# Residual projection in 512-column pieces, inverse roots by a GpSimd power, gate weight splits two blocks later, last gate parts of 512, 384 and 128 columns

## The chip, the cores and the metric

The kernel runs on one core of a Trainium2 chip. The metric is the device time of one execution in microseconds (us), the median of several executions. The engines are named as in the profile: PE is the matrix engine (PEld its weight loads), DVE the vector engine, ACT the scalar engine, POOL the GpSimd engine, and SP the engine whose queue starts most of the transfers.

## The reference, cut to what matters

512 tokens of width 1024 go through one block. The residual stream is `h`.

```python
xn = rms_norm(h, g_mix)
proj = xn @ w_in                                  # 1024 -> 2048
h = h + concat([y_conv, y_pool]) @ w_o            # the residual projection, 1024 -> 1024
h = h + peer_ffn(rms_norm(h, g_ffn), ...)         # 16384 experts, top 16 per head and token
gate = sigmoid(rms_norm(h, g_ple) @ w_ple_gate)   # the gate, 1024 -> 1024
h = h + gate * (p @ w_ple_proj)
return rms_norm(h, g_final)

def rms_norm(x, g):
    return x * rsqrt(mean(x * x) + 1e-6) * g
```

`rms_norm` occurs four times for every token. Each time it needs one inverse root per token, so one column of 128 numbers for a tile of 128 tokens.

## The kernel before, in words

Tokens are in 4 tiles of 128. Almost every product is made of three matmuls: both operands are split into a rounded high part and a low part (`xH`, `xL`), and `mm3` adds high by high, high by low and low by high in one accumulator (lines L126, L130 and L128). A split (`split_ld`, L98) is a copy on ACT (L99) and a subtraction on DVE (L100).

The program runs in this order.

- **Start.** `h` is loaded and `norm_rows` scales the four tiles by their inverse root. Four small projections of `p` (`ple`, L190) run on PE meanwhile, then `h` is transposed and the input projection `w_in` begins. This part is in the order in which it is written (a manual schedule).
- **Middle, in an order that a scheduler chooses.** The rest of `w_in`, the convolution and the pooling, which leave their result in `mixH` and `mixL`. Then the **residual projection** (L307 to L319): `w_o` comes in four pieces of 256 columns by all eight chunks of 128 rows. Every piece is loaded to `wraw`, split to `wH` and `wL` (two buffers each), and used for the four token tiles, 24 matmuls of 256 columns each, after which DVE adds the accumulator to `h`. Four more `ple`, the norm of the new `h`, its transposes, the query projection, the top-k search, and the scores of experts (accumulators `acc`) follow.
- **Expert values, written by hand in order again.** From L795 on, a loop over 128 blocks of 128 experts. Block `n` is multiplied into six accumulators `o` (three token tiles by two halves, 18 matmuls of 512 columns). The loop body prepares later blocks: ACT and DVE split the expert weights `wH`, `wL` of block `n + 2` and the rows `vH`, `vL` of block `n + 2`, and SP loads `vraw` of block `n + 5`. The fourth token tile does not use this path: POOL gathers its 256 rows of experts one at a time (L540, indirect DMA) and DVE adds them (L564). In blocks 76 to 104 of this loop the gate weight comes in as eight chunks: `gate_dma` (L731) loads one chunk to `tH` (two buffers) at the end of every fourth block, and `gate_split` (L741) splits it one block later (L862).
- **Tail.** For the four tiles in the order 3, 0, 1, 2: `tail_norm` (norm), `tail_T` (transposes), `tail_gate` (gate projection in parts, sigmoid on ACT, product and sum on DVE, square sum on ACT for the last norm) and `tail_out` (inverse root, scaling, store). Three tiles do the gate in two parts of 512 columns (`HS`), the last one in three of 512, 256 and 256 (`QS`, L747).

The **inverse root** (`rsqrt`, L102) is one ACT square root, then a reciprocal and one Newton step in four DVE operations on 128x1. Before it, DVE turns the sum of squares into the mean plus epsilon (L118, and L907 or L909 in the tail). In the tail ACT changes between the tables of the square root and of the sigmoid. In the last part of the last tile a dummy square root (L900) brings its table load ahead of the square.

ACT, DVE and PE take their instructions in order, so an instruction that waits holds back everything behind it on its engine.

Of the kernel before, what the change touches and what calls it, by code (L numbers as in the profile page):

```python
# [7 lines left out]
F32 = mybir.dt.float32  # L8
# [8 lines left out]
P = 128  # L17
# [37 lines left out]

SEGS = [(0, 1, 16), (1, 1, 8), (2, 1, 5), (3, 1, 4), (4, 1, 3), (5, 3, 2), (8, 8, 1)]
NCAND = sum(n * b for _, n, b in SEGS)


@with_exitstack  # L60
def block_kernel(ctx: ExitStack, tc: tile.TileContext, x, pT_in, g_cols, w_in, conv_w, pool_w,
# [31 lines left out]
    eidx = consts.tile([P, P], I32, name="eidx")  # L93
    gate3 = consts.tile([P, P], F32, name="gate3")
    xrow = consts.tile([P, D], F32, name="xrow")
    consts.tile([P, 64], F32, name="lpad")

    def split_ld(src, hi, lo):  # L98
        nc.scalar.activation(hi, src, AF.Copy)  # L99
        nc.vector.tensor_tensor(lo, src, hi.bitcast(F32), op=OP.subtract)  # L100

    def rsqrt(ms):  # L102
        sq = small.tile([P, 1], F32, name="sq")
        nc.scalar.activation(sq, ms, AF.Sqrt)
        r = small.tile([P, 1], F32, name="r")
        nc.vector.reciprocal(r, sq)
        t = small.tile([P, 1], F32, name="nt")
        nc.vector.scalar_tensor_tensor(t, r, ms, r, op0=OP.mult, op1=OP.mult)
        nc.vector.tensor_scalar(t, t, -0.5, 1.5, op0=OP.mult, op1=OP.add)
        r2 = small.tile([P, 1], F32, name="r2", bufs=4)  # L110
        nc.vector.tensor_tensor(r2, r, t, op=OP.mult)
        return r2

    def rstd(src, scratch):
        ss = small.tile([P, 1], F32, name="ss")
        nc.scalar.activation(scratch, src, AF.Square, accum_out=ss)
        ms = small.tile([P, 1], F32, name="ms")
        nc.vector.tensor_scalar(ms, ss, 1.0 / D, EPS, op0=OP.mult, op1=OP.add)  # L118
        return rsqrt(ms)

    def mm3(ps, lh, ll, rh, rl, start, stop):
        mm3_pair([(ps, lh, ll, rh, rl)], start, stop)
# [43 lines left out]
    def piece_hl():  # L166
        return (wpool.tile([P, DC, 256], F32R, name="wH"), wpool.tile([P, DC, 256], F32R, name="wL"))

    def piece(w, c0):
        raw = piece_dma(w, c0)  # L170
        hl = piece_hl()
        split_ld(raw, *hl)
        return hl
# [27 lines left out]
    start.enter_context(tc.manual_schedule())  # L201
    warm = consts.tile([P, 1], F32, name="warm")
    nc.vector.memset(warm, 1.0)
    nc.scalar.activation(warm, warm, AF.Sqrt)
    ple_w(0)
    nc.sync.dma_start(h[:, 0], x[:P])
    ident = const("ident", ident_in, [P, P])
# [67 lines left out]
    for k, pc in enumerate(order):  # L275
        w = pieces.pop(pc)
        if 0 < k < len(order) - 1:
            pieces[order[k + 1]] = piece(w_in, order[k + 1] * 256)
        elif k:
            pieces["o0"] = piece(w_o, 0)  # L280
        both = projT(w, xh, xl) if k else first
        for b in range(2):
            ps = both[b]
            blk = 2 * pc + b
            kind, g = divmod(blk, 4)
            if kind == 3:
                pool_group(g, ps)
            elif kind == 1:
                cbuf[g] = wk.tile([P, T], F32, name="cb")
                nc.scalar.activation(cbuf[g], ps, AF.Copy)  # L290
            elif kind == 2:
                z = wk.tile([P, T + 2], F32, name="zb", bufs=1)
                nc.vector.memset(z[:, 0:1], 0.0)
                nc.vector.memset(z[:, T + 1:], 0.0)
                nc.vector.tensor_tensor(z[:, 1:T + 1], cbuf[g], ps, op=OP.mult)
                y = wk.tile([P, T], F32, name="yb")
                nc.vector.tensor_scalar(y, z[:, 0:T], cw[:, g, 0:1], None, op0=OP.mult)
                nc.vector.scalar_tensor_tensor(y, z[:, 1:T + 1], cw[:, g, 1:2], y, op0=OP.mult, op1=OP.add)
                nc.vector.scalar_tensor_tensor(y, z[:, 2:T + 2], cw[:, g, 2:3], y, op0=OP.mult, op1=OP.add)
                zbuf[g] = y  # L300
            else:
                m = wk.tile([P, T], F32, name="cm", bufs=1)
                nc.vector.tensor_tensor(m, zbuf[g], ps, op=OP.mult)
                split_ld(m, mixH[:, g], mixL[:, g])

    corder = [4, 5, 6, 7, 0, 1, 2, 3]
    for qd in range(4):  # L307
        w = pieces.pop("o%d" % qd)
        if qd < 3:
            pieces["o%d" % (qd + 1)] = piece(w_o, (qd + 1) * 256)  # L310
        else:
            pieces["q0"] = piece(w_q, 0)
        for t in range(NT):
            ps = psum.tile([P, T], F32, name="acc", bufs=4)
            ts = slice(t * P, (t + 1) * P)
            for ci, c in enumerate(corder):
                mm3(ps[:, :256], mixH[:, c, ts], mixL[:, c, ts], w[0][:, c], w[1][:, c], ci == 0, ci == DC - 1)
            hs = h[:, t, qd * 256:(qd + 1) * 256]
            nc.vector.tensor_tensor(hs, hs, ps[:, :256], op=OP.add)  # L319

    for t in range(NT):
        ple(t, 1)
# [421 lines left out]
            split_ld(raw[:, hf * 512:(hf + 1) * 512], *wg(hf, c))  # L744

    HS = [slice(0, 512), slice(512, 1024)]
    QS = [slice(0, 512), slice(512, 768), slice(768, 1024)]  # L747
    st_t, fin_t = {}, {}

    def tail_norm(t):  # L750
# [44 lines left out]
    for n in range(NE - LAST):  # L795
        m = n + LAG
        i = n - NS
        if m < NR:
            r = RATES[0]
        elif m < NG:  # L800
            r = RATES[1]
        elif m < NS:
            r = RATES[2]
        else:
            if left is None:
                left = 2 * P - done[0]
# [36 lines left out]
        gather(max(0, q - 2))  # L843
        if fu:
            gelu(m, ps)
            if m % 2:
                w_mult(m - 1)
                w_h(m - 1)
                w_l(m - 1)
        if n == NE - LAST - 1:  # L850
            for k in range(n + LAG + 1, NE):
                w_mult(k)
                w_h(k)
                w_l(k)
            for k in range(n + 3, NE):
                v_h(k)
                v_l(k)
            tail_norm(ND)
        mix(n, range(ND))
        if 16 <= i < 48 and i % 4 == 0:  # L860
            gate_dma((i - 16) // 4)
        if 17 <= i < 49 and i % 4 == 1:  # L862
            gate_split((i - 16) // 4)
        if i == 48:
            nc.sync.dma_start(gpb, bcast(g_ple))
            nc.sync.dma_start(gfin, bcast(g_final))
# [17 lines left out]
    def tail_gate(t, bank, parts, obuf):  # L884
# [1 line left out]
        sg = wq.tile([P, D], F32, name="aq")  # L886
        o_ = vb.tile([P, D], F32, name=obuf)
        ss = small.tile([P, 3], F32, name="ss2")
        m0 = None
        for n, s in enumerate(parts):  # L890
            hf, o = divmod(s.start, 512)
            w = s.stop - s.start
# [3 lines left out]
                mm3(ps, hi[:, c], lo[:, c], wh[:, o:o + w], wl[:, o:o + w], c == 0, c == DC - 1)  # L896
            yield
            nc.scalar.activation(sg[:, s], ps, AF.Sigmoid)
            if n == len(parts) - 1 == 2:
                nc.scalar.activation(warm, warm, AF.Sqrt)  # L900
            nc.vector.tensor_tensor(sg[:, s], sg[:, s], pl[:, s], op=OP.mult)
            nc.vector.tensor_tensor(sg[:, s], sg[:, s], h3[:, s], op=OP.add)
            nc.scalar.activation(ps, sg[:, s], AF.Square, accum_out=ss[:, n:n + 1])
            nc.vector.tensor_tensor(o_[:, s], sg[:, s], gfin[:, s], op=OP.mult)
            m1 = small.tile([P, 1], F32, name="ms3", bufs=6)
            if n == 0:
                nc.vector.tensor_scalar(m1, ss[:, 0:1], 1.0 / D, EPS, op0=OP.mult, op1=OP.add)  # L907
            else:
                nc.vector.scalar_tensor_tensor(m1, ss[:, n:n + 1], 1.0 / D, m0, op0=OP.mult, op1=OP.add)  # L909
            m0 = m1  # L910
        fin_t[t] = o_, m0

    def tail_out(t):
        o_, ms_ = fin_t[t]
        r = rsqrt(ms_)
        nc.vector.tensor_scalar(o_[:, HS[0]], o_[:, HS[0]], r, None, op0=OP.mult)
        nc.sync.dma_start(out[t * P:(t + 1) * P, HS[0]], o_[:, HS[0]])
        if t < ND - 1 or t == ND:
# [84 lines left out]
```

## Time and profile before

| what | value |
|---|---|
| median of 3 runs | 1442.31 us (1441.92 to 1448.14) |
| the profiled execution's own time | 1441.66 us |
| its span, from the first to the last instruction | 1439.9 us |
| PE busy | 1421.2 us (99%) |
| DVE busy | 1137.6 us (79%) |
| ACT busy | 613.1 us (43%) |
| POOL busy | 381.2 us (26%) |
| granted TensorE clock, mean | 0.998 of 2.4 GHz |

The span is 1.8 us shorter than the execution's own time, and that execution is 0.65 us under the median of the runs. Matmuls overlap in the profile: a 512-column one is shown with 390 ns, while the next starts 227 ns later. What PE can do is therefore read from the distance between starts.

### The profile page before, as it was taken

The page shows a single profiled execution, that of the slowest core. Times are in us where ns is not written, and L with a number is a line of the kernel's source. Part 1 is how long each engine was busy: PE and PEld are TensorE (multiplying, and loading weights), DVE is VectorE, ACT ScalarE, POOL GpSimd, SP SyncE. Part 2 cuts the span into 40 slices and gives each one's busy share as a digit, 9 for nine tenths or more (in the row PEclk, how much of TensorE's full clock was granted, in tenths as well). Part 3 has the DMA queues.
Part 4 walks back from the last instruction along what each step waited for, and adds up shares of the span by engine and source line. Part 5 has one row for each costly group of instructions (what it writes and reads, how often), then busy time and mean ns, then how long its engine had stood idle before and what let it go on. Part 6 is the DMA issues. An engine that isn't in the chain of part 4 may idle for free.

```text
span 1439.9 us, 20603 instructions
## 1 busy us (share of the span) xinstructions
PE 1421.2 (99%) x7785; PEld 1268.5 (88%) x7785; DVE 1137.6 (79%) x2078; ACT 613.1 (43%) x864; POOL 381.2 (26%) x260
## 2 busy tenths in 40 slices
PE   8999999999999999999999999999999999999997
PEld 5789888999999999998999999999998888778886
DVE  5653679899999988869988779887887777777665
ACT  5321533344565666663333333333333333334345
POOL 0000000002121241116766456444443123332000
PEclk9999999999999999999999999999999999999999
DMA  8233730158688989989998989898878989998621
GB/s 293 88 102 103 254 113 30 31 182 293 218 300 304 312 296 319 292 314 329 384 360 324 380 310 371 330 344 331 337 280 310 330 311 338 330 331 321 242 72 73
DMA packets 152083, 380.99 MB, mean 265 GB/s; under 512 B 10928, under 2 KB 72240, under 8 KB 151728
## 3 DMA queue, kind: packets, MB, share of 16 engines
q1 hardware_dynamic: 72400, 211.36, 41.3%
q0 software_dynamic: 36864, 134.23, 25.5%
q10 hardware_dynamic: 42720, 34.08, 7.2%
q8 instruction: 61, 1.00, 0.3%
q14 instruction: 38, 0.31, 0.1%
HBM read 339.53 MB, written 40.11 MB: 264 GB/s over the span
## 4 chain that ended last, share of the span: by engine, by line
PE 92%; DVE 3%; DMA 3%; issue 1%; ACT 1%; SPq 0%; DVEq 0%
PE acc L128 13%; PE acc L130 12%; PE acc L126 12%; PE o L130 11%; PE o L128 11%; PE o L126 11%; PE u L130 5%; PE u L126 5%; PE u L128 5%; DMA tH<-in_w_gate 2%; PE g L474 2%; PE g L475 2%; DVE vL L608 1%; PE acc L194 1%; PE tp L520 1%
## 5 line engine op out<-in xcount | busy, mean ns | idle before, releaser
L540 POOL DMA_INDIRECT gr<-in_u_rows,eidx x128 | 198.0, 1547 | 640.3 <-DVE tsm L393 329.9
L540 POOL DMA_INDIRECT gr<-in_v_rows,eidx x128 | 183.0, 1430 | 294.9 <-DVE xrow L564 284.3
L128 PE MATMUL o<-vL,wH 128*128 128x512 f32 x768 | 237.8, 391 | 1.4 <-DVE vL L608 1.4
L126 PE MATMUL o<-vH,wH 128*128 128x512 f32 x768 | 238.2, 391 | 1.0 <-ACT wH L691 1.0
L130 PE MATMUL o<-vH,wL 128*128 128x512 f32 x768 | 238.0, 391 | 0.8 <-DVE wL L696 0.6
L602 ACT ACTIVATE vH<-vraw 128x1024 fp32r<-128x1024 f32 x128 | 135.3, 1058 | 216.6 <-PE o L130 170.0
L608 DVE TENSOR_TENSOR vL<-vraw,vH 128x1024 fp32r<-128x1024 f32 x128 | 156.3, 1221 | 64.0 <-ACT vH L602 63.9
L128 PE MATMUL acc<-xL,uH 128*128 128x384 f32 x608 | 206.1, 339 | 0.0
L126 PE MATMUL acc<-xH,uH 128*128 128x384 f32 x608 | 204.1, 336 | 0.0
L130 PE MATMUL acc<-xH,uL 128*128 128x384 f32 x608 | 203.6, 335 | 0.0
L584 ACT ACTIVATE uH<-uraw 128x1024 fp32r<-128x1024 f32 x128 | 135.1, 1057 | 124.6 <-PE acc L128 105.6
L128 PEld LDWEIGHTS o<-vL,wH 128*128 128x128 f32 x768 | 144.3, 188 | 33.2 <-DVE vL L608 2.3
L130 PEld LDWEIGHTS o<-vH,wL 128*128 128x128 f32 x768 | 144.3, 188 | 32.6 <-DVE wL L696 2.2
L590 DVE TENSOR_TENSOR uL<-uraw,uH 128x1024 fp32r<-128x1024 f32 x128 | 155.4, 1217 | 20.8 <-ACT uH L584 20.3
L126 PEld LDWEIGHTS o<-vH,wH 128*128 128x128 f32 x768 | 143.5, 188 | 28.4 <-ACT wH L691 1.8
L564 DVE SCALAR_TENSOR_TENSOR xrow<-gr,gate,xrow 128x1024 f32<-128x1024 f32 x128 | 164.2, 1283 | 5.1 <-DMA xrow<-h_d 4.6
L560 DVE SCALAR_TENSOR_TENSOR gr<-gr,xrow 128x1024 f32<-128x1024 f32 x128 | 154.2, 1216 | 4.5 <-DMA gr<-in_u_rows,eidx 4.5
L130 PE MATMUL u<-xH,uL 128*128 128x384 f32 x416 | 139.6, 336 | 0.0
L126 PE MATMUL u<-xH,uH 128*128 128x384 f32 x416 | 139.6, 336 | 0.0
L128 PE MATMUL u<-xL,uH 128*128 128x384 f32 x416 | 139.3, 335 | 0.0
L130 PEld LDWEIGHTS acc<-xH,uL 128*128 128x128 f32 x608 | 114.3, 188 | 0.0
L128 PEld LDWEIGHTS acc<-xL,uH 128*128 128x128 f32 x608 | 114.2, 188 | 0.0
(214 smaller groups left out, 2329.6 us busy)
## 6 DMA issues: line engine op xcount, KB each, us to landing
uraw<-in_u_blk SPq DMA_DIRECT2D x128, 512.0 KB, 5.1
vraw<-in_v_rows SPq DMA_DIRECT2D x128, 512.0 KB, 5.5
G_d<-stage ACTq DMA_DIRECT2D x12, 1664.0 KB, 12.3
gq<-G_d SPq DMA_DIRECT2D x26, 768.0 KB, 7.0
A_d<-a ACTq DMA_DIRECT2D x17, 768.0 KB, 4.9
aq<-A_d SPq DMA_DIRECT2D x17, 768.0 KB, 9.4
wraw<-in_w_in SPq DMA_DIRECT2D x8, 1024.0 KB, 5.5
wraw<-in_w_q SPq DMA_DIRECT2D x8, 1024.0 KB, 5.6
```

The source lines that it names most:

```text
L126: nc.tensor.matmul(ps, lh, rh, start=start, stop=False)
L128: nc.tensor.matmul(ps, lh, rl, start=False, stop=False)
L130: nc.tensor.matmul(ps, ll, rh, start=False, stop=stop)
L474: nc.tensor.matmul(o, oh[:, 1, n, :, e], gg[:, 0, n, :, e], start=True, stop=False)
L475: nc.tensor.matmul(o, oh[:, 1, n, :, e], gg[:, 1, n, :, e], start=False, stop=True)
L540: nc.gpsimd.indirect_dma_start(out=g, out_offset=None, in_=table, in_offset=bass.IndirectOffsetOnAxis(ap=eidx[:, k:k + 1], axis=0))
L560: ins = nc.vector.scalar_tensor_tensor(g, g, 1.0, xrow, op0=OP.mult, op1=OP.mult, accum_out=act[:, k:k + 1])
L564: ins = nc.vector.scalar_tensor_tensor(accg, g, gate3[:, k - P:k - P + 1], accg, op0=OP.mult, op1=OP.add)
L584: nc.scalar.activation(ublk[i][1], ublk[i][0], AF.Copy)
L590: nc.vector.tensor_tensor(ublk[i][2], raw, uh.bitcast(F32), op=OP.subtract)
L602: nc.scalar.activation(vblk[n][1], vblk[n][0], AF.Copy)
L608: nc.vector.tensor_tensor(vblk[n][2], raw, vh.bitcast(F32), op=OP.subtract)
```

## The change

Four edits.

1. The residual projection takes `w_o` in pieces of 512 columns by four row chunks, first chunks 4 to 7 and then 0 to 3 of each half. The four accumulators of a half stay open over two pieces. There are 192 matmuls of 512 columns in place of 384 of 256, and 8 additions to `h` of 512 columns in place of 16 of 256.
2. `rsqrt` is one DVE addition of epsilon and one POOL `TENSOR_TENSOR` with the power -0.5. The factor 1/1024 moves into the scale of ACT's square. The square root, the Newton step and the dummy square root go away. In the tail the root now follows at the end of `tail_gate`, no longer at the start of `tail_out`.
3. `gate_split` of a chunk stands two blocks later. The loads stay where they are.
4. The last tile's gate parts are 512, 384 and 128 columns.

```diff
+OG = (slice(4, 8), slice(0, 4))
...
-    def rsqrt(ms):
-        sq = small.tile([P, 1], F32, name="sq")
-        nc.scalar.activation(sq, ms, AF.Sqrt)
-        r = small.tile([P, 1], F32, name="r")
-        nc.vector.reciprocal(r, sq)
-        t = small.tile([P, 1], F32, name="nt")
-        nc.vector.scalar_tensor_tensor(t, r, ms, r, op0=OP.mult, op1=OP.mult)
-        nc.vector.tensor_scalar(t, t, -0.5, 1.5, op0=OP.mult, op1=OP.add)
-        r2 = small.tile([P, 1], F32, name="r2", bufs=4)
-        nc.vector.tensor_tensor(r2, r, t, op=OP.mult)
-        return r2
+    def rsqrt(ms, more):
+        r = small.tile([P, 1], F32, name="r2", bufs=4)
+        m = small.tile([P, 1], F32, name="me")
+        nc.vector.tensor_scalar(m, ms, more, None, op0=OP.add)
+        nc.gpsimd.tensor_tensor(r, m, power, op=OP.pow)
+        return r

     def rstd(src, scratch):
-        ss = small.tile([P, 1], F32, name="ss")
-        nc.scalar.activation(scratch, src, AF.Square, accum_out=ss)
         ms = small.tile([P, 1], F32, name="ms")
-        nc.vector.tensor_scalar(ms, ss, 1.0 / D, EPS, op0=OP.mult, op1=OP.add)
-        return rsqrt(ms)
+        nc.scalar.activation(scratch, src, AF.Square, scale=D ** -0.5, accum_out=ms)
+        return rsqrt(ms, EPS)
...
+    def piece_o(k):
+        hf, g = divmod(k, 2)
+        raw = wpool.tile([P, DC, 256], F32, name="wraw")
+        nc.sync.dma_start(wide(raw), w_o[:, hf * 512:(hf + 1) * 512].rearrange("(c p) n -> p c n", p=P)[:, OG[g]])
+        hl = piece_hl()
+        split_ld(raw, *hl)
+        pieces["o%d" % k] = [wide(a) for a in hl]
...
-    corder = [4, 5, 6, 7, 0, 1, 2, 3]
-    for qd in range(4):
-        w = pieces.pop("o%d" % qd)
+    both_hf = []
+    for k in range(4):
+        hf, g = divmod(k, 2)
+        w = pieces.pop("o%d" % k)
...
+        if g == 0:
+            both_hf = [psum.tile([P, T], F32, name="acc", bufs=4) for _ in range(NT)]
         for t in range(NT):
-            ps = psum.tile([P, T], F32, name="acc", bufs=4)
             ts = slice(t * P, (t + 1) * P)
-            for ci, c in enumerate(corder):
-                mm3(ps[:, :256], mixH[:, c, ts], mixL[:, c, ts], w[0][:, c], w[1][:, c], ci == 0, ci == DC - 1)
-            hs = h[:, t, qd * 256:(qd + 1) * 256]
-            nc.vector.tensor_tensor(hs, hs, ps[:, :256], op=OP.add)
+            for n in range(4):
+                c = OG[g].start + n
+                mm3(both_hf[t], mixH[:, c, ts], mixL[:, c, ts], w[0][:, n], w[1][:, n], g == 0 and n == 0,
+                    g == 1 and n == 3)
+            if g:
+                hs = h[:, t, hf * 512:(hf + 1) * 512]
+                nc.vector.tensor_tensor(hs, hs, both_hf[t], op=OP.add)
...
-    QS = [slice(0, 512), slice(512, 768), slice(768, 1024)]
+    QS = [slice(0, 512), slice(512, 896), slice(896, 1024)]
...
-        if 17 <= i < 49 and i % 4 == 1:
+        if 19 <= i < 51 and i % 4 == 3:
             gate_split((i - 16) // 4)
...
             nc.scalar.activation(sg[:, s], ps, AF.Sigmoid)
-            if n == len(parts) - 1 == 2:
-                nc.scalar.activation(warm, warm, AF.Sqrt)
...
-            nc.scalar.activation(ps, sg[:, s], AF.Square, accum_out=ss[:, n:n + 1])
+            nc.scalar.activation(ps, sg[:, s], AF.Square, scale=D ** -0.5, accum_out=ss[:, n:n + 1])
...
-        fin_t[t] = o_, m0
+        fin_t[t] = o_, rsqrt(ss[:, len(parts) - 1:len(parts)], m0)
```

How the order on the engines changes at two places. First ACT in the loop over expert blocks, where the first gate chunk (`tH`) is split into `xH` and `uraw`; `vraw` is a block of expert rows, `aq` a group of four blocks of expert weights. Before:

```order
L691 ACTIVATE wH_11047<-aq_10920 128x768
L602 ACTIVATE vH_11073<-vraw_10988 128x1024
L602 ACTIVATE vH_11101<-vraw_11017 128x1024
L691 ACTIVATE wH_11103<-aq_10920 128x768
L602 ACTIVATE vH_11144<-vraw_11051 128x1024
L99 ACTIVATE xH_11129<-tH_11139 128x512
L99 ACTIVATE uraw_11131<-tH_11139 128x512
L602 ACTIVATE vH_11180<-vraw_11077 128x1024
L691 ACTIVATE wH_11182<-aq_11039 128x768
L602 ACTIVATE vH_11208<-vraw_11107 128x1024
```

The same place with the change, where `aq_10777` is the group that `aq_11039` is before:

```order
L703 ACTIVATE wH_10841<-aq_10658 128x768
L614 ACTIVATE vH_10882<-vraw_10789 128x1024
L614 ACTIVATE vH_10914<-vraw_10815 128x1024
L703 ACTIVATE wH_10916<-aq_10777 128x768
L614 ACTIVATE vH_10942<-vraw_10845 128x1024
L101 ACTIVATE xH_10867<-tH_10877 128x512
L101 ACTIVATE uraw_10869<-tH_10877 128x512
L614 ACTIVATE vH_10974<-vraw_10886 128x1024
L703 ACTIVATE wH_10976<-aq_10777 128x768
```

Before, the split came in front of the first `wH` of the new group; now that `wH` and two more `vH` come ahead of it. DVE's half of the split moves by the same two blocks, and SP's order is as it was.

Second POOL at the start of the program, where `r` is a tile's inverse root and `power` the column of -0.5. With the change:

```order
L999 MEMSET const-uint8-127 128x1
L1006 UNCONDITIONAL_BRANCH
L108 ISA
L108 TENSOR_TENSOR r2_125<-me_126,power_83 128x1
L108 TENSOR_TENSOR r2_133<-me_134,power_83 128x1
L108 TENSOR_TENSOR r2_147<-me_148,power_83 128x1
L108 TENSOR_TENSOR r2_161<-me_162,power_83 128x1
```

Before, the first gather followed the branch at once. Now an `ISA` row, which names line L108 as the powers do, and the powers stand ahead of it; four more powers follow for the second norm, and eight stand behind the last gather.

## Rows read from the trace of the kernel before

**Rows 1.** The chain that ended last, its shares of the span by engine.
```profile
PE 92%; DVE 3%; DMA 3%; issue 1%; ACT 1%; SPq 0%; DVEq 0%
```

**Rows 2.** Timeline of PE, residual projection: start, duration, operation, form, count.
```profile
108.96 0.62 PE L126 MATMUL acc<-xH,wH 128*128 128x512 f32 x2
...
111.68 0.28 PE L126 MATMUL acc<-wH,mixH 128*128 128x256 f32 x1
...
157.64 0.28 PE L130 MATMUL acc<-wH,mixL 128*128 128x256 f32 x1
```

**Rows 3.** Timeline of ACT, expert blocks; in brackets the idle time before and what ended it.
```profile
1170.68 1.06 ACT L602 ACTIVATE vH<-vraw 128x1024 fp32r<-128x1024 f32 x1 [2.29 <-PE o L130]
...
1209.49 0.63 ACT L99 ACTIVATE xH<-tH 128x512 fp32r<-128x512 f32 x1 [5.10 <-DMA tH<-in_w_gate]
...
1219.64 1.06 ACT L602 ACTIVATE vH<-vraw 128x1024 fp32r<-128x1024 f32 x1 [1.25 <-PE o L130]
1228.20 0.63 ACT L99 ACTIVATE xH<-tH 128x512 fp32r<-128x512 f32 x1 [7.49 <-DMA tH<-in_w_gate]
...
1263.38 0.63 ACT L99 ACTIVATE xH<-tH 128x512 fp32r<-128x512 f32 x1 [6.00 <-DMA tH<-in_w_gate]
```

**Rows 4.** Timeline of PE, the two holes in the expert blocks.
```profile
1231.18 0.61 PE L130 MATMUL o<-vH,wL 128*128 128x512 f32 x2
...
1234.85 0.62 PE L126 MATMUL o<-vH,wH 128*128 128x512 f32 x2
...
1265.69 0.61 PE L130 MATMUL o<-vH,wL 128*128 128x512 f32 x2
...
1272.78 0.62 PE L126 MATMUL o<-vH,wH 128*128 128x512 f32 x2
```

**Rows 5.** GB/s in 40 slices; then a stretch: engines' busy us, clock, DMA share, GB/s.
```profile
GB/s 293 88 102 103 254 113 30 31 182 293 218 300 304 312 296 319 292 314 329 384 360 324 380 310 371 330 344 331 337 280 310 330 311 338 330 331 321 242 72 73
...
1178.80:1211.50 32.70, 32.70 (x146) 27.06 (x145) 25.19 (x27) 13.66 (x16) 10.29 (x6) 1.00 0.93 345
```

**Rows 6.** Timelines of DVE and ACT at the start of the program.
```profile
9.19 0.15 DVE L118 TENSOR_SCALAR ms<-ss 128x1 f32<-128x1 f32 x1 [8.20 <-ACT xs L116]
...
16.49 0.75 DVE L158 TENSOR_SCALAR xs<-h,r 128x1024 f32<-128x1024 f32 x1
...
17.80 0.68 ACT L141 ACTIVATE xH<-g,gcol 128x512 fp32r<-128x512 f32 x1
```

**Rows 7.** POOL: a small write; all gathers of one kind, ns min/median/max.
```profile
0.33 0.12 POOL L992 MEMSET const-uint8-127<- 128x1 uint8 x1
...
L540 POOL DMA_INDIRECT gr<-in_u_rows,eidx x128: 935/1681/2580, 330.4 to 836.8; - x128
```

**Rows 8.** Timelines of PE, ACT and DVE, last tile.
```profile
1425.99 0.28 PE L126 MATMUL o<-uraw,tH 128*128 128x256 f32 x1
...
1427.07 0.69 DVE L901 TENSOR_TENSOR aq<-aq,vraw 128x512 f32<-128x512 f32 x1 [0.19 <-ACT aq L898]
...
1428.59 0.60 ACT L903 ACTIVATE o<-aq 128x512 f32<-128x512 f32 x1 [1.54 <-DVE aq L902]
...
1431.94 0.38 ACT L898 ACTIVATE aq<-u 128x256 f32<-128x256 f32 x1 [0.83 <-PE u L130]
1432.34 1.28 ACT L900 ACT_TABLE_LOAD   x1
1432.35 0.43 DVE L901 TENSOR_TENSOR aq<-aq,vraw 128x256 f32<-128x256 f32 x1 [1.06 <-ACT aq L898]
...
1434.05 0.19 ACT L903 ACTIVATION_READ_ACCUMULATOR u<-aq 128x1 f32 x1
...
1435.53 0.72 ACT L922 ACTIVATE vH<-vH,r 128x512 f32<-128x512 f32 x1 [0.86 <-DVE r L111]
```

**Rows 9.** Timelines of DVE and PE, first norm of the tail.
```profile
1376.79 1.42 DVE L760 SCALAR_TENSOR_TENSOR gq<-xrow,r,gpb 128x512 f32<-128x512 f32 x2
...
1380.23 1.03 PE L877 MATMUL u<-ident,gq 128*128 128x128 f32 x8
```

More of the change, by code (lines that the diff above doesn't have):

```diff
@@ L95, in block_kernel @@
     xrow = consts.tile([P, D], F32, name="xrow")
-    consts.tile([P, 64], F32, name="lpad")
+    power = consts.tile([P, 1], F32, name="power")
+    consts.tile([P, 104], F32, name="lpad")
     def split_ld(src, hi, lo):
@@ L167, in piece_hl, with wide @@
         return (wpool.tile([P, DC, 256], F32R, name="wH"), wpool.tile([P, DC, 256], F32R, name="wL"))
+    def wide(a):
+        return a.rearrange("p c n -> p (c n)").rearrange("p (c n) -> p c n", n=512)
+    def piece_o(k):
[5 more added lines that the diff above has]
+        pieces["o%d" % k] = [wide(a) for a in hl]
     def piece(w, c0):
@@ L203, in block_kernel @@
     nc.vector.memset(warm, 1.0)
-    nc.scalar.activation(warm, warm, AF.Sqrt)
+    nc.vector.memset(power, -0.5)
+    nc.scalar.activation(warm, warm, AF.Square)
     ple_w(0)
@@ L279, in block_kernel @@
         elif k:
-            pieces["o0"] = piece(w_o, 0)
+            piece_o(0)
         both = projT(w, xh, xl) if k else first
@@ L304, in block_kernel @@
                 split_ld(m, mixH[:, g], mixL[:, g])
-    corder = [4, 5, 6, 7, 0, 1, 2, 3]
-    for qd in range(4):
-        w = pieces.pop("o%d" % qd)
-        if qd < 3:
-            pieces["o%d" % (qd + 1)] = piece(w_o, (qd + 1) * 256)
+    both_hf = []
+    for k in range(4):
+        hf, g = divmod(k, 2)
+        w = pieces.pop("o%d" % k)
+        if k < 3:
+            piece_o(k + 1)
         else:
             pieces["q0"] = piece(w_q, 0)
+        if g == 0:
+            both_hf = [psum.tile([P, T], F32, name="acc", bufs=4) for _ in range(NT)]
         for t in range(NT):
-            ps = psum.tile([P, T], F32, name="acc", bufs=4)
             ts = slice(t * P, (t + 1) * P)
-            for ci, c in enumerate(corder):
-                mm3(ps[:, :256], mixH[:, c, ts], mixL[:, c, ts], w[0][:, c], w[1][:, c], ci == 0, ci == DC - 1)
-            hs = h[:, t, qd * 256:(qd + 1) * 256]
-            nc.vector.tensor_tensor(hs, hs, ps[:, :256], op=OP.add)
+            for n in range(4):
[5 more added lines that the diff above has]
+                nc.vector.tensor_tensor(hs, hs, both_hf[t], op=OP.add)
     for t in range(NT):
@@ L888, in tail_gate @@
         ss = small.tile([P, 3], F32, name="ss2")
-        m0 = None
+        m0 = EPS
         for n, s in enumerate(parts):
@@ L898, in tail_gate @@
             nc.scalar.activation(sg[:, s], ps, AF.Sigmoid)
-            if n == len(parts) - 1 == 2:
-                nc.scalar.activation(warm, warm, AF.Sqrt)
             nc.vector.tensor_tensor(sg[:, s], sg[:, s], pl[:, s], op=OP.mult)
             nc.vector.tensor_tensor(sg[:, s], sg[:, s], h3[:, s], op=OP.add)
-            nc.scalar.activation(ps, sg[:, s], AF.Square, accum_out=ss[:, n:n + 1])
+            nc.scalar.activation(ps, sg[:, s], AF.Square, scale=D ** -0.5, accum_out=ss[:, n:n + 1])
             nc.vector.tensor_tensor(o_[:, s], sg[:, s], gfin[:, s], op=OP.mult)
[L905 to L910, printed above, removed]
-        fin_t[t] = o_, m0
+            if n < len(parts) - 1:
+                m1 = small.tile([P, 1], F32, name="ms3", bufs=6)
+                nc.vector.tensor_scalar(m1, ss[:, n:n + 1], m0, None, op0=OP.add)
+                m0 = m1
+        fin_t[t] = o_, rsqrt(ss[:, len(parts) - 1:len(parts)], m0)
     def tail_out(t):
-        o_, ms_ = fin_t[t]
-        r = rsqrt(ms_)
+        o_, r = fin_t[t]
         nc.vector.tensor_scalar(o_[:, HS[0]], o_[:, HS[0]], r, None, op0=OP.mult)
```

## The prediction

> **What bounds the kernel.** I read the chain that ended last first: PE carries 92% of the span [rows 1]. So an edit gains where it takes matmul time away, where it closes a hole in PE's stream, or behind the last matmul. Then I read PE's timeline at the residual projection, for the distance between starts [rows 2], and PE's and ACT's timelines in the expert blocks, where PE has holes [rows 3, 4]. Last come the two ends of the program, where PE waits for other engines [rows 6, 8]. The numbers below are against the profiled execution: 1441.66 us, with a span of 1439.9.
>
> **Residual projection.** Its 384 matmuls of 256 columns run from 111.68 to 157.64 + 0.12 = 157.76 [rows 2]: 46.08 us, 0.120 each, with no hole. The 512-column matmuls just ahead go from 108.96 to 111.68 for six pairs [rows 2], 0.2267 each. The change has 192 of these: 43.52 us. **Gain 2.56 us.** A piece now lasts 48 x 0.2267 = 10.9 us instead of 11.5, and its splits on ACT and DVE have that time; the last mixed chunks (2 and 3) are needed one piece later than before. The four accumulators of the second half are freed tile by tile, three tiles ahead. I cost all this at nothing; it is covered by PE's own work, and without that cover one split would show.
>
> **Gate splits.** ACT reaches a gate split and stands until the chunk lands; the next blocks' `vH` and `wH` are queued behind it. A block lasts 18 x 0.2267 = 4.08 us. The wait of 5.10 us cost nothing: from the copy at 1170.68 to that at 1219.64 is 48.96 us, exactly 12 blocks [rows 3]. The waits of 7.49 and 6.00 us did [rows 3]: PE needs 3.67 us for four pairs of matmuls from 1231.18 to 1234.85, and 7.09 for seven from 1265.69 to 1272.78 [rows 4]. At 0.4533 per pair they are due 1.81 and 3.17, so 1.86 and 3.92 us are lost, 5.78 together. Two blocks later is 8.16 us later. The longest wait is 7.49, so none is left, and one of up to 5 us would still be free. The load of a chunk stays at its place on SP, and its buffer is free long before the next but one. **Gain 5.78 us.** Late next would be the transfers; that is a rival below.
>
> **The root on POOL.** It replaces a square root and four DVE steps by one addition and one power. No row shows a power on POOL. The nearest below is a write of one column, 0.12 us; the nearest above a gather's descriptors, 1.68 in the median [rows 7]. I take P = 0.5 us, nearer to the write, since both touch one column, and keep 0.12 and 1.68 for the range. A DVE step on one column takes 0.15 [rows 6]. The Trainium skill (GPSIMD Engine Reference, section 4.1) says elementwise work belongs on VectorE, GpSimd being about half as fast; by it P would be an estimated 0.3, twice the DVE step, and the gain 9.1 us instead of 8.9. No row here shows it.
>
> - *Start.* DVE does the addition, then waits for the power, then scales the tile, four times in order. With 0.1 us (estimate) for each of two handoffs the last scaling starts at 9.19 + 4 x (0.15 + 0.2 + P) + 3 x 0.75 = 12.84 + 4P. Before it started at 16.49 [rows 6]. P = 0.5 gives 14.84, earlier, but the first copy to `xH` at 17.80 [rows 6] stands behind ACT's other copies, so I take **0**. P above 0.91 makes it later; P = 1.68 gives 19.56, 3.1 us lost.
> - *Middle norm.* PE does four output tiles of `ple` between the projection and the last transposes, and they cover the root at every P of this range. **0**.
> - *Tail.* PE has the last mixing and the other tiles' gates to do while a norm runs. **0**, up to the last tile.
>
> **The last tile.** Its 512-column part ends on PE at 1425.99 [rows 8]. Before, 48 matmuls of 0.12 end at 1431.75, the last sigmoid starts at 1431.94, and the scaling at 1435.53 [rows 8], 3.59 us later, with a table load of 1.28 in between. Now the 384-column part takes 24 x 0.1733 (between 0.12 and 0.2267), to 1430.15, and its sigmoid starts at 1430.34. By widths between those shown (ACT 0.60 and 0.38, DVE 0.69 and 0.43 [rows 8]) its steps are sigmoid 0.49, product 0.56, sum 0.56, square 0.49, readout 0.19 [rows 8], 2.3 us. ACT is in order, so the last sigmoid can't start before 1432.6, **later** than before although its part is narrower. PE is done with the 24 matmuls of 128 columns at 1431.75 at the pace 0.067 that the wider ones extrapolate to, or at 1433.0 at the pace of 256 columns, 0.12. From the sigmoid on: 0.27 + 0.30 + 0.30 + 0.27 + 0.19 + 0.15, 0.3 for handoffs (estimate), and P: 1.78 + P. The scaling starts at 1432.6 + 1.78 + 0.5 = 1434.9 instead of 1435.53: **gain 0.6 us**. With P = 0.12 it is 1.0; with P = 1.68 and the slow matmuls (sigmoid at 1433.2) 1.1 lost. The stores behind are the same.
>
> **Sum.** 2.56 + 5.78 + 0 + 0.6 = 8.94 us, so 1441.66 - 8.94 = 1432.7. The median of the three runs is 0.65 above the profiled execution; I put the forecast between the two bases, at **1433.0**. The bounds of P give 1432.3 (gain 1.0 at the end) and, with 3.1 lost at the start and 1.1 at the end, 1437.5.
>
> **Rivals.**
>
> *The first power is late.* The order has an `ISA` row ahead of the first power, naming its line, that the kernel before lacks. If that fetches code, it may run from the branch on, with more than 8 us until the first sum at 9.19 [rows 6], hidden; or the first power may have to wait for it. With P = 0.5 the start has 16.49 - 14.84 = 1.65 us to spare. A code fetch is a transfer, and for one ACT was seen waiting 7.49 us [rows 3]. Of that 5.84 would show: 1432.7 + 5.8 = 1438.6. Against it: the first gather, POOL's first larger instruction, shows no such cost, as the longest of all took 2.58 us [rows 7]. The Trainium skill (GPSIMD Engine Reference, section 2.1) states that the first call into freshly loaded code pays about 6 us that the profile shows as no instruction; by it this rival gives an estimated 1437. Nothing here shows it. Chance 0.17, with a long P.
>
> *The gate's holes come back as late transfers.* Without holes the loads come faster. The stretch without a hole took 345 GB/s at a DMA share of 0.93, and PE lost nothing there; slices of the span reach 384 [rows 5]. That speaks against it. If the holes return in full, 1432.7 + 5.8 = 1438.5. Chance 0.07.
>
> *Slower: the power's code is fetched twice, at the start and again after the 256 gathers, at L us each.* In the tail the scaled norm was ready at 1376.79 + 1.42 = 1378.21 and PE takes it at 1380.23 [rows 9]: 2.0 to spare, and up to 1.5 more since a table load goes there too. The total is -8.94 + (L - 1.65) + (L - 3.5), above zero from L = 7.1 and over 7.2 us, or 0.5% (about what a measurement of this kernel can tell from no change), from L = 10.7. At 12 us the time is 1441.7 + 9.9 = 1451.6. For it speaks that the powers of the start and of the tail have all gathers between them; against, that the order shows one `ISA` row there and none in the tail. Chance 0.09, of which 0.07 is slower by over 0.5%.
>
> **How the numbers follow.** The forecast keeps 0.67. Its gain of 8.94 passes 7.2 unless P is near its upper bound, which takes about 0.04 off; a short delay in the first rival leaves some 0.03 on that side. So faster 0.66, same 0.27 (the two rivals in between and the long P), slower 0.07. The range goes from 1430.5, somewhat under the lower bound because I took the start at 0, to 1440.0, which holds the first two rivals with the 0.65 between the bases; it leaves out the slower one.
>
> **What would show it.** Right: the residual projection lasts 43.5 us with starts 0.227 apart; no ACT wait for `tH` and blocks 4.08 apart throughout; powers under 0.9 us on POOL; the first `xH` near 17.8; the last scaling near 1426.5. Wrong: a DVE wait of several us for POOL ahead of the first scaled tile; ACT idle for `vraw` or `tH` with PE holes in the expert blocks; a power over 1 us; a second wait of PE for POOL's root in the tail.

## The result, and the profile after

The changed kernel takes 1433.72 us, the median of ten runs (1432.33 to 1444.74). The kernel before, run beside it, took 1444.70 (1440.78 to 1448.14). The ratio is 0.9939, with a 95% interval from 0.9914 to 0.9964: faster. The forecast was 1433.0, in a range from 1430.5 to 1440.0. So by the medians measured side by side the gain is 11.0 us. Beside the experiments below, on three chips, the kernel before had medians from 1439.0 (one run) to 1440.6; the changed kernel was not run beside those, and against them its 1433.72 would be a gain of 5 to 7 us only. So where medians of different sets of runs are compared below, the ratio to the kernel before beside each says more. The profiled executions are 1441.66 and 1432.93 us long, 8.73 apart, and the two traces are read against each other.

The page of the changed kernel gives the chain that ended last. PE has gone from 92% [rows 1] to 98%, and DVE and DMA hardly appear:

```profile
PE 98%; DMA 1%; ACT 1%; DVE 0%; issue 0%; POOLq 0%; SPq 0%; ACTq 0%
```

Timeline of PE: first and last matmul of the residual projection, and the first of the next projection (before, [rows 2]).

```profile
111.27 0.39 PE L121 MATMUL acc<-wH,mixH 128*128 128x512 f32 x1
...
154.56 0.40 PE L125 MATMUL acc<-wH,mixL 128*128 128x512 f32 x1
...
164.03 1.23 PE L121 MATMUL acc<-xH,wH 128*128 128x512 f32 x4 [0.45 <-ACT xH L136]
```

From 111.27 to 154.56 + 0.23 = 154.79 are 43.52 us, 192 x 0.2267.

The power's line with all its instructions (nanoseconds: shortest, median, longest, then first and last start), and below it the timelines of DVE, POOL and ACT at the start (before, [rows 6]).

```profile
L108 POOL TENSOR_TENSOR r<-me,power x16: 547/549/565, 9.5 to 1426.2; 128x1 f32<-128x1 f32 x16
...
L108 POOLq MODIFY_POOL_CONFIG  x2: 11/11/11, 0.7 to 0.8; - x2
```

```profile
9.29 0.15 DVE L107 TENSOR_SCALAR me<-ms 128x1 f32<-128x1 f32 x1 [8.29 <-ACT xs L113]
9.53 0.55 POOL L108 TENSOR_TENSOR r<-me,power 128x1 f32<-128x1 f32 x1 [9.10 <-DVE me L107]
...
14.77 0.15 DVE L107 TENSOR_SCALAR me<-ms 128x1 f32<-128x1 f32 x1 [0.79 <-ACT xs L113]
...
15.59 0.75 DVE L153 TENSOR_SCALAR xs<-h,r 128x1024 f32<-128x1024 f32 x1 [0.66 <-POOL r L108]
...
16.54 0.60 ACT L201 ACTIVATE pleo<-acc 128x512 f32<-128x512 f32 x1 [1.12 <-PE acc L200]
...
17.34 0.68 ACT L136 ACTIVATE xH<-g,gcol 128x512 fp32r<-128x512 f32 x1
```

A power takes 0.55 us, the first as long as the others. The last tile is scaled at 15.59 instead of 16.49, and ACT's first copy to `xH` starts at 17.34 instead of 17.80, behind ACT's copy of the last `ple`, which waited for PE.

Timeline of ACT in the expert blocks (before, [rows 3]): no wait for `tH`, and the copies to `vH` stand 4.08 apart.

```profile
1171.98 1.06 ACT L614 ACTIVATE vH<-vraw 128x1024 fp32r<-128x1024 f32 x1 [3.02 <-PE o L125]
...
1176.07 1.06 ACT L614 ACTIVATE vH<-vraw 128x1024 fp32r<-128x1024 f32 x1 [2.28 <-issue]
1177.03 0.62 ACT L101 ACTIVATE xH<-tH 128x512 fp32r<-128x512 f32 x1
...
1180.14 1.06 ACT L614 ACTIVATE vH<-vraw 128x1024 fp32r<-128x1024 f32 x1 [1.98 <-issue]
```

PE alone in a stretch of both kernels, the kernel before first (length, PE's busy us and instructions, granted clock, DMA share, GB/s). The holes [rows 4] are gone, with the slightly lower clock around them.

```profile
1160.00:1300.00 140.00, 137.42 (x594) 0.99 0.91 334
```

```profile
1160.00:1300.00 140.00, 140.00 (x619) 1.00 0.92 351
```

The last tile (before, [rows 8]): start of the 384-column part, and first and last start of the 128-column part.

```profile
1417.40 0.33 PE L121 MATMUL o<-uraw,tH 128*128 128x384 f32 x1
...
1421.58 0.22 PE L121 MATMUL u<-uraw,tH 128*128 128x128 f32 x1
...
1424.10 0.28 PE L125 MATMUL u<-uH,tL 128*128 128x128 f32 x1
```

Behind them, on ACT and POOL:

```profile
1424.41 0.28 ACT L910 ACTIVATE aq<-u 128x128 f32<-128x128 f32 x1 [0.24 <-PE u L125]
...
1426.23 0.55 POOL L108 TENSOR_TENSOR r<-me,power 128x1 f32<-128x1 f32 x1 [10.26 <-DVE me L107]
1426.81 0.72 ACT L929 ACTIVATE vH<-vH,r 128x512 f32<-128x512 f32 x1 [0.97 <-POOL r L108]
```

From the end of the 512-column part to the scaling it is 1426.81 - 1417.40 = 9.41 us; before it was 1435.53 - 1425.99 = 9.54 [rows 8].

So the 8.72 us between the two last scalings come from: 0.41 at the start (first matmul of the residual projection, 111.68 to 111.27), 2.56 in that projection, 5.8 in the gate splits' stage and 0.13 in the last tile, less 0.2 in small amounts between. The 0.41 is not the root's. In the kernel before and in every run with a single power, the first copy to `xH` starts 1.42 or 1.43 us behind the start of the last of PE's 16 `ple` matmuls. That matmul starts at 16.37 before, at 15.91 here, and anywhere from 14.89 to 16.54 in the experiments that leave the start as it is, so that the first copy comes anywhere from 16.32 to 17.96. PE starts these matmuls about 0.85 us apart at first and 0.43 apart later, and the pace changes behind another one of them in each execution; why is not shown.

### The profile page after: what moved, and what is told of

Read it like the earlier page. It is cut to its first block, busy times and chain, and to the rows that moved or that the text cites. A ratio compares the mean times of both kernels' runs of the same rounds, so it can differ in the third digit from the quotient of the medians.

```text
span 1431.2 us, 20153 instructions
## 1 busy us (share of the span) xinstructions
PE 1415.8 (99%) x7593; PEld 1258.9 (88%) x7593; DVE 1127.8 (79%) x2007; ACT 600.7 (42%) x839; POOL 380.0 (27%) x276
## 4 chain that ended last, share of the span: by engine, by line
PE 98%; DMA 1%; ACT 1%; DVE 0%; issue 0%; POOLq 0%; SPq 0%; ACTq 0%
PE o L125 13%; PE o L121 13%; PE o L123 13%; PE acc L123 13%; PE acc L125 12%; PE acc L121 12%; PE u L125 5%; PE u L121 5%; PE u L123 5%; PE g L486 2%; PE g L487 2%; PE acc L200 1%; PE tp L532 1%; DMA wp<-in_w_proj 0%; DMA vraw<-in_v_rows 0%; PE u L889 0%
## 5 line engine op out<-in xcount | busy, mean ns | idle before, releaser
L552 POOL DMA_INDIRECT gr<-in_v_rows,eidx x128 | 170.6, 1333 | 301.6 <-DVE xrow L576 290.9
```

Of the source, the lines that this page charges most:

```text
L552: nc.gpsimd.indirect_dma_start(out=g, out_offset=None, in_=table, in_offset=bass.IndirectOffsetOnAxis(ap=eidx[:, k:k + 1], axis=0))
```

## The experiments

**One part undone at a time.** Four kernels, each the changed one with one part put back.

The projection in pieces of 256 columns again:

```diff
-            piece_o(0)
+            pieces["o0"] = piece(w_o, 0)
...
-                mm3(both_hf[t], mixH[:, c, ts], mixL[:, c, ts], w[0][:, n], w[1][:, n], g == 0 and n == 0,
-                    g == 1 and n == 3)
+                mm3(ps[:, :256], mixH[:, c, ts], mixL[:, c, ts], w[0][:, c], w[1][:, c], ci == 0, ci == DC - 1)
```

> The changed kernel with the residual projection as before (four pieces of 256 columns). Theory (the 0.120 us start distance of 256-column matmuls against 0.227 of 512 is all of it): the projection lasts 46.1 us instead of 43.5 and the span is 2.6 us longer than the changed kernel's 1431.2, so 1433.8. Rival (the gain there is taken back by the norm behind it, which PE has to wait for in either form): the span moves by less than 0.5 us although the projection takes 2.6 us longer.

Measured: 1434.86 us (six runs), ratio to before 0.9971 [0.9955, 0.9986]. PE's timeline has the projection from 110.25 to 156.20 + 0.12, 46.07 us:

```profile
110.25 0.28 PE L121 MATMUL acc<-wH,mixH 128*128 128x256 f32 x1
...
156.20 0.28 PE L125 MATMUL acc<-wH,mixL 128*128 128x256 f32 x1
...
165.60 1.20 PE L121 MATMUL acc<-xH,wH 128*128 128x512 f32 x4 [0.50 <-ACT xH L136]
```

From that first matmul to the next projection's first it is 165.60 - 110.25 = 55.35 us, against 52.76 in the changed kernel: 2.59 lost. Behind that the two traces differ by 0.14 up to the last tile's sigmoid. The span, 1432.9, is only 1.7 longer than the changed kernel's, because this execution reached the projection 1.02 earlier. The term is confirmed.

The gate splits back one block behind the loads:

```diff
-        if 19 <= i < 51 and i % 4 == 3:
+        if 17 <= i < 49 and i % 4 == 1:
```

> The changed kernel with the gate splits one block after their load, as before. Theory (ACT stands for the chunk and holds vH and wH back): ACT waits of 3 to 8 us for tH come back, eight of them, those over 5.5 us leave holes on PE, and the span is 3 to 6 us longer, 1434 to 1437. Rival (the holes came from transfers that were late for another reason): the waits come back but PE has no hole, and the span stays at 1431 to 1432.

Measured: 1437.60 us (ten runs), ratio 0.9983 [0.9971, 0.9995]. ACT's waits in the stretch 1150 to 1320 (us in all, times, longest) are back, and a window of PE shows holes, though small ones; a third view, PE's timeline, shows a wait outside the stage:

```profile
ACT xH L101 <- DMA tH<-in_w_gate: 38.2, 8, 6.5
```

```profile
1260.00:1300.00 40.00, 39.58 (x174) 1.00 0.94 353
```

```profile
644.13 0.73 PE L125 MATMUL o<-vH,wL 128*128 128x512 f32 x2 [2.76 <-DVE wL L708]
```

The stage is taken from the same `vH` copy to the last tile's first sigmoid, the changed kernel first, then this one:

```profile
1164.10 1.06 ACT L614 ACTIVATE vH<-vraw 128x1024 fp32r<-128x1024 f32 x1 [3.29 <-PE o L125]
...
1417.60 0.60 ACT L910 ACTIVATE aq<-o 128x512 f32<-128x512 f32 x1 [2.57 <-PE o L125]
```

```profile
1166.94 1.06 ACT L614 ACTIVATE vH<-vraw 128x1024 fp32r<-128x1024 f32 x1 [3.29 <-PE o L125]
...
1421.99 0.60 ACT L910 ACTIVATE aq<-o 128x512 f32<-128x512 f32 x1 [2.58 <-PE o L125]
```

It is 255.05 us long instead of 253.50, so about 1.54 longer. In the kernel before, such waits cost 5.8 [rows 3, 4]: their sum was 40.7 us against 38.2, the longest 7.49 against 6.5. The sums are nearly alike and the costs are not, so the cost hangs on how late single chunks come. The rest of this profile's loss is the wait at 644 and a granted clock of 0.91 in the 20 us around it; the changed kernel waits 0.93 us there, at 1.00. How much of the 3.9 us between the two medians (of different sets of runs) is the splits' was not separated.

The last parts of 512, 256 and 256 columns:

```diff
-    QS = [slice(0, 512), slice(512, 896), slice(896, 1024)]
+    QS = [slice(0, 512), slice(512, 768), slice(768, 1024)]
```

> The changed kernel with the last tile's gate in parts of 512, 256 and 256 columns. Theory (128-column matmuls start 0.111 us apart, nearly as far as 256-column ones with 0.120, so the 384 and 128 columns cost PE 6.8 us where 256 and 256 cost 5.8): from the first matmul behind the 512 part to the last scaling 8.8 us instead of 9.41, the span 0.6 us shorter, 1430.6. Rival (the narrower last part pays, because its steps behind PE are shorter): 9.8 us or more, the span 0.4 us longer.

Measured: 1432.36 us (four runs), ratio 0.9946 [0.9926, 0.9965]. PE's and DVE's rows of the last tile:

```profile
1417.89 0.28 PE L121 MATMUL o<-uraw,tH 128*128 128x256 f32 x1
...
1426.72 0.48 DVE L923 TENSOR_SCALAR vH<-vH,r 128x512 f32<-128x512 f32 x1 [0.72 <-POOL r L108]
```

1426.72 - 1417.89 = 8.83 us instead of 9.41. The new part sizes cost 0.58 us in the last tile. The span, 1431.1, is only 0.1 shorter, as this execution reached the projection 0.39 later, and the times alone don't part it from the changed kernel.

The old root everywhere, square root and Newton step, with the dummy square root of the last part and a square root, not a square, as ACT's first function:

```diff
-        nc.gpsimd.tensor_tensor(r, m, power, op=OP.pow)
-        return r
+        sq = small.tile([P, 1], F32, name="sq")
+        nc.scalar.activation(sq, m, AF.Sqrt)
+        r = small.tile([P, 1], F32, name="r")
+        nc.vector.reciprocal(r, sq)
...
+        return r2
```

> The changed kernel with the inverse root as before: square root on ACT, reciprocal and Newton step on DVE, dummy square root in the last part. Theory (the root on POOL is off the path everywhere but at the end): first copy to xH at 17.3 to 17.8 as in other runs, the tail as long up to the last tile, and the last stretch (first matmul behind the 512 part to last scaling) 10.5 us instead of 9.41, because table load and Newton steps are back; span 1.1 us longer. Rival (the earlier start of the changed kernel, 0.46 us at the first xH, is the power's): the first xH goes back to 17.8 and the span is 1.5 us longer.

Measured: 1440.19 us (ten runs), ratio 1.0003 [0.9989, 1.0016]: 6.5 us above the changed kernel's median, where 1.1 to 1.5 were expected. Most of the loss stood where no root runs. The timelines of PE, the changed kernel first, then this one, show the projections' matmuls from the same operation to the same operation:

```profile
70.47 0.62 PE L121 MATMUL acc<-xH,wH 128*128 128x512 f32 x2
...
92.22 0.62 PE L121 MATMUL acc<-xH,wH 128*128 128x512 f32 x2
```

```profile
70.36 0.63 PE L128 MATMUL acc<-xH,wH 128*128 128x512 f32 x2
...
92.75 0.63 PE L128 MATMUL acc<-xH,wH 128*128 128x512 f32 x2
```

21.75 us for 96 matmuls are 0.2266 each; 22.39 are 0.2333. The clock is granted in full in both. The groups by form show which matmuls (busy us, mean ns of one): `acc<-xH,wH` has 401 ns here and 395 in the changed kernel, while `o<-vH,wH` and `acc<-wH,mixH` stay at 390 and 389.

```profile
L128 PE MATMUL acc<-xH,wH 128*128 128x512 f32 x256 | 83.3, 401 | 0.5 <-ACT xH L143 0.5
...
L128 PE MATMUL o<-vH,wH 128*128 128x512 f32 x768 | 237.4, 390 | 0.0
...
L128 PE MATMUL acc<-wH,mixH 128*128 128x512 f32 x64 | 24.9, 389 | 0.0
```

What differs is the place in SBUF, the on-chip memory where the tiles lie. The old root's small tiles lie on the left, at its low addresses, ahead of `xH` and `xL`, and push them and all that follows up by 192 bytes; the weights of the projections and of the gate lie on the right, at its high end, and stay. In `acc<-xH,wH` one operand moved and the other didn't; in the other two both moved or neither.

**The place alone.** The change has a line that the prediction passed over, a filler tile on the left that is never read:

```diff
-    consts.tile([P, 64], F32, name="lpad")
+    consts.tile([P, 104], F32, name="lpad")
```

With it `xH` starts at the same byte, 13312, in the kernel before and in the changed one, although the tiles of the root went. The next two runs part root and place. The old root with the filler cut by 192 bytes (104 to 56 numbers):

> The old root of sqrt and Newton steps in all places, as in the run before it, but the filler tile lpad cut from 104 to 56 numbers, so that xH, xL and all that follows on the left of SBUF start where they do in the changed kernel (they had moved by 192 bytes). Theory: 6.1 us of the 7.3 that the old root seemed to cost came from that move, since 768 projection matmuls of 512 columns with xH or xL started 0.2333 us apart instead of 0.2267 and the last gate's with tH too; with the place restored they are 0.2267 apart again, and the root itself is worth 1.2 us: 1434.9 us. Rival: the old root costs 7 us by itself: 1441 us, and 0.2333 stays.

Measured: 1434.26 us (twelve runs), ratio 0.9971 [0.9961, 0.9982], 5.93 us under the run with 104 numbers there. The projections' matmuls start 0.2268 us apart again (from 70.56 to 92.33, 96 of them). The place was nearly all of it. From the end of the 512-column part (PE's row of the next part) to the scaling it is 1433.26 - 1422.81 = 10.45 us, 1.04 more than with the power:

```profile
1422.81 0.33 PE L128 MATMUL o<-uraw,tH 128*128 128x384 f32 x1
...
1433.06 0.16 DVE L115 TENSOR_TENSOR r<-r,nt 128x1 f32<-128x1 f32 x1
...
1433.26 0.72 ACT L938 ACTIVATE vH<-vH,r 128x512 f32<-128x512 f32 x1 [0.87 <-DVE r L115]
```

At the start this run shows what the power takes away. PE was done early with `ple` (its last matmul started at 14.67) and then stood for the last scaled tile (PE's waits: us in all, times, longest; then ACT's timeline):

```profile
PE g L141 <- DVE xs L160: 1.5, 1, 1.5
```

```profile
17.44 0.69 ACT L143 ACTIVATE xH<-g,gcol 128x512 fp32r<-128x512 f32 x1 [0.77 <-PE g L141]
```

The first copy to `xH` starts 2.77 us behind that matmul instead of 1.43, so here the old root cost 1.3 us; with the filler at 104 numbers it was 1.86 behind, and the old root cost 0.4. In the kernel before, `ple` ended later and hid the root.

The profiled execution was itself 5.2 us above the median, since a wait of PE for `wL` at 645 took 3.56 us there, with a granted clock of 0.73 in the 10 us around it:

```profile
640.00:650.00 10.00, 6.44 (x21) 0.73 0.41 134
```

The changed kernel with the filler back at 64 numbers, 160 bytes lower, and nothing else:

> The changed kernel with the filler tile lpad back at 64 numbers, nothing else: xH and xL and what follows start 160 bytes lower. Theory (a move of the left side against the weights on the right slows these matmuls): projections at 0.2333 us instead of 0.2267, 768 x 0.0067 = 5.1 us, and the last gate's some 0.9: 1439.7 us. Rival (lpad is filler without effect): 1433.7 us, as the changed kernel, and 0.2267.

Measured: 1438.82 us (eleven runs), ratio 1.0002 [0.9992, 1.0011]. That line alone is worth 5.1 us, nearly all that the changed kernel's 1433.72 gains on the median of before beside this run (1439.46). The span is 5.8 longer, of which 0.5 is a later start. The projections' timeline, 22.40 us for 96 matmuls:

```profile
70.62 0.63 PE L121 MATMUL acc<-xH,wH 128*128 128x512 f32 x2
...
93.02 0.63 PE L121 MATMUL acc<-xH,wH 128*128 128x512 f32 x2
```

The residual projection itself, whose operands both lie on the right, takes 43.55 us here and doesn't notice.

Then three more places, by the same line (lpad of 112, 120 and 168 numbers), one run each, and a fourth, 136 numbers, on top of the parts of 512, 256 and 256 columns:

> The changed kernel with lpad at 112 numbers: the left side 32 bytes higher, the weights of the projections on the right unmoved. If any unequal start of the two operands is slow: projections 0.2333 us apart. If only starts off a coarser grid matter: still 0.2267.

> The changed kernel with lpad at 120 numbers: the left side 64 bytes higher. If any unequal start of the two operands is slow: projections 0.2333 us apart. If 64 bytes is the grid: 0.2267.

> The changed kernel with lpad at 168 numbers: the left side 256 bytes higher. If any unequal start of the two operands is slow: projections 0.2333 us apart. If 256 bytes or less is the grid: 0.2267.

> The changed kernel with the last parts of 512, 256 and 256 columns, as in the third run, and the left side 128 bytes higher (lpad at 136 numbers). Theory: if 128 bytes is as good as 256, projections are 0.2267 us apart and the time is again about 0.6 us under the changed kernel's, 1433.1 us; if only 256 is good, they are 0.2333 apart and the time 1439 us. Either way the stretch from the last 512-column part's end to the last scaling is 8.8 us (9.41 in the changed kernel).

The distance between starts of `acc<-xH,wH`'s stream, over 96 or 102 matmuls each (the times come from several sets of runs):

| left side moved by | lpad | us between starts | time, us |
|---|---|---|---|
| 0 | 104 | 0.2266 | 1433.72 |
| 0 | 56, old root | 0.2268 | 1434.26 |
| +32 bytes | 112 | 0.2333 | 1438.35 (one run) |
| +64 | 120 | 0.2289 | 1439.41 (one run) |
| +128 | 136 | 0.2333 | 1436.65 (parts of 256) |
| +192 | 104, old root | 0.2333 | 1440.19 |
| +256 | 168 | 0.2266 | 1433.18 (one run) |
| -160 | 64 | 0.2333 | 1438.82 |

Two rows of the move by 64, as an instance (102 matmuls, 23.35 us):

```profile
69.95 0.62 PE L121 MATMUL acc<-xH,wH 128*128 128x512 f32 x2
...
93.30 0.62 PE L121 MATMUL acc<-xH,wH 128*128 128x512 f32 x2
```

Of the moves tried, only the one by 256 bytes is as good as none; 64 bytes costs a third of the others. The run at 64 bytes is late for other reasons too: PE waited 2.0 us once for a tile (`gg`) that DVE makes, and the start was 0.6 later. The fourth run's last tile took 1437.99 - 1429.22 = 8.77 us, as expected of its parts; its median is 1436.65, 2.4 us better than a slow pace was expected to give, with a ratio of 0.9973 [0.9961, 0.9985]. Its trace is of the slowest of the twelve executions, 1444.17 us, and why the median lies lower stays open. Whether what counts is the difference between the two operands' starts or the place of `xH` alone was not tried by itself. For the difference speaks `o<-vH,wH`: with the old root its `vH` lay 192 bytes higher too, but so did its weights, and its 390 ns stayed.

**How far the root is covered.** Each power issued three times:

```diff
-        nc.gpsimd.tensor_tensor(r, m, power, op=OP.pow)
+        for _ in range(3):
+            nc.gpsimd.tensor_tensor(r, m, power, op=OP.pow)
```

> Each root's power issued three times on GpSimd, so 1.65 us instead of 0.55. Theory: the root lies on the path at the start (three powers of 1.65 us plus hand-offs and 0.8 us apart: last xs near 19.0 instead of 15.59, PE some 3 us later) and at the very end (1.1 us): span near 1435.3, time 1437.5 at most. Rival: the start's copies on ACT bind anyway and only the end's 1.1 us shows: span near 1432.3.

Measured: 1438.93 us (ten runs), ratio 1.0007 [0.9992, 1.0021], span 1436.6: the theory's way, but 1.3 us above its span and 1.4 above its highest time. PE now waits twice ahead of the transposes, and runs at a lower clock behind that (timeline, then PE's window):

```profile
17.52 0.33 PE L135 MATMUL g<-ident,xs 128*128 128x128 f32 x1 [1.95 <-DVE me L107]
...
19.45 0.75 DVE L154 TENSOR_SCALAR xs<-h,r 128x1024 f32<-128x1024 f32 x1 [1.92 <-POOL r L109]
...
20.25 0.47 PE L135 MATMUL g<-ident,xs 128*128 128x128 f32 x1 [2.40 <-DVE xs L154]
```

```profile
14.00:30.00 16.00, 11.65 (x56) 0.89 0.72 257
```

The residual projection starts 4.45 us later (115.72), where some 3 were expected. The stretch from there to the next projection is 52.76 us in both kernels: the middle norm's root is covered. The last tile takes 1.18 more. So the start and the end are where the power's length counts; a root of 1.8 us would have taken back 5.6 of the 8.7 us.

**One block later is enough.** The splits one block later than before, not two:

```diff
-        if 19 <= i < 51 and i % 4 == 3:
+        if 18 <= i < 50 and i % 4 == 2:
```

> The gate weight's splits one block later than before the change instead of two. Theory (the hole on PE comes only when the wait on ACT exceeds what the queue of finished copies covers; one block is 5.4 us, waits were 5 to 7.5 us): waits of up to 2 to 3.4 us remain on ACT but PE keeps busy, time as the changed kernel, 1433.7 us. Rival: each remaining wait reaches PE: up to 3 us more, 1436.7 us.

Measured: 1432.77 us (ten runs), ratio 0.9965 [0.9948, 0.9982]. ACT's timeline shows not even the rest of a wait for `tH`, and the copies stand 4.08 apart:

```profile
1188.88 1.06 ACT L614 ACTIVATE vH<-vraw 128x1024 fp32r<-128x1024 f32 x1 [3.02 <-PE o L125]
...
1190.58 0.61 ACT L101 ACTIVATE xH<-tH 128x512 fp32r<-128x512 f32 x1
...
1192.96 1.06 ACT L614 ACTIVATE vH<-vraw 128x1024 fp32r<-128x1024 f32 x1 [1.25 <-issue]
```

The expectation took a block for 5.4 us and so left waits; a block is 4.08. The waits were up to 7.49 us [rows 3], so a block of 4.08 alone would have left 3.4. The trace shows two more things: ACT comes to the split 6.86 to 7.14 us after the issue of the chunk's load, where before it came at most 2.4 us after it, and a chunk lands 5.7 to 6.8 us after its issue, where it took 4.3 to 8.1. What makes the landings more even was not tried by itself.

## Why the prediction was right, and where not

- **Residual projection, 2.56 us: right.** 43.52 us, and 46.07 with the old pieces back. No split showed.
- **Gate splits, 5.78 us: right for the two profiled executions**, where 5.8 came back. Shown as a mechanism by putting the splits back, but its size is no constant: in that execution the stage lost 1.54 us, a quarter. The term was read from one execution whose two longest waits were 7.49 and 6.00.
- **The power, 0.5 us: 0.55.** The price lay near the one-column write, as taken. The Trainium skill (GPSIMD Engine Reference, section 4.1) has GpSimd about half as fast as VectorE on elementwise work with two inputs; here the power took 0.55 us and DVE's product of two columns 0.16 (the row `r<-r,nt` above), another operation, but more than three times as fast, and the measurement decides.
- **Start, 0: right for this execution**, with a last scaling at 15.59 where 14.84 was reckoned. The fourth sum waited 0.79 us for ACT's square, which the formula of equal steps left out. The first copy to `xH` did stand behind other work, PE's `ple` and ACT's copy of it, and that cover is not always there: with the old root at the same place in SBUF it was short by 1.3 us. For a long power the formula gives 20.04 at 1.80 us, 3.6 later than before. With three powers the scaling came at 19.45, but PE reached the projection 4.0 later than before, as its granted clock was 0.89 around the two waits.
- **Middle, 0: right**, at three powers too. **Tail, 0:** no root of the power's stood in the chain ahead of the last tile.
- **The last tile, 0.6 us: mis-sized, 0.13.** The step that failed is the pace of the 128-column matmuls. They were put between 0.067 and 0.12 us, with ACT's order as the bound at 1432.6. Measured, 24 of them take from 1421.58 to 1424.20, 0.11 each, little less than the 0.12 of 256 columns. So the sigmoid starts 7.01 us behind the 512-column part instead of 6.61, and it waits for PE, by 0.24 us, not for ACT. The 384-column part, 4.18 us, was right, and the steps behind the sigmoid took 2.40 instead of 2.28. The Trainium skill (TensorE: Matmul & The Clock Gate, section on the back-to-back issue gap) gives 0.081 us for 128 columns in a stream with weight loads; this trace does not agree. The root's gain and the parts' loss nearly cancel there. With the old root the new parts take 10.45 us where the old took 9.54, 0.91 lost; the power gives back 1.04; 0.13 is left.
- **The first rival, a late first power: did not happen in any run.** The instruction that it rested on lasts 11 ns at 0.7 us, and the first power, at 9.53, is no longer than the rest. Whether something loads unseen in between is open: anything over by 9.5 would not show.
- **The second rival, late transfers: fell.** 351 GB/s at a share of 0.92, and PE busy for all of the 140 us.
- **The slower rival, the code fetched twice: fell.** No power in the tail was longer than 0.57 us, and PE never waits for POOL's root there.
- **The sum, 8.94 us against 8.72 between the last scalings, is closer than its terms.** The 0.41 that the start gave, by PE's pace in `ple`, stands in for the 0.47 that the last tile lacked; that is luck. So is a part of the median's closeness, 1433.72 to 1433.0, as the gate term was read from one execution and is smaller in another.
- **What no step named:** each pace of 0.2267 was taken over from the kernel before, as if it went with the width alone. In the projections around the residual one it held because the filler tile kept `xH` where it was. With 64 numbers there, the same four edits would have come to 1438.82 us, and the forecast would have been 5.8 too low.

## What to carry to other kernels

An edit that removes or adds small tiles also moves every tile behind them: compare the distance between starts of the same matmuls ahead of and behind the edit, in a stage that the edit doesn't touch, before a gain or a loss is put down to it. A wait ahead of a stream is priced from the longest waits of several executions, and by what PE's clock does behind it, not from the sum of the waits. Halving a last part pays only while its matmuls get shorter with it.

## What was not expected of the hardware

- The same 512-column matmul, at the same granted clock, starts every 0.2266 us or every 0.2333, by where its operand `xH` lies: with its weights unmoved, 32, 128, 192 bytes up or 160 down cost 0.0067 us a matmul, 64 up cost 0.0023, and 256 up nothing.
- With a wait of PE of 3.56 us the granted clock was 0.73 in the 10 us around it and 0.93 in the next 10, and that execution was 5.2 us over its median; with one of 0.93 us at the same place it stayed at 1.00.
- 24 matmuls of 128 columns took 2.62 us, as many of 256 columns 24 x 0.12 = 2.88, each with its weight load.
